# A hybrid encoder layer on one core: the triangular inverses split into halves, and decays from one scan of logarithms

## The chip, the core and the metric

The kernel runs on one core of a Trainium2 chip. A core has a matrix engine (PE, with its weight loads as PEld), three engines for elementwise work (DVE, ACT and POOL), a queue SP that here issues nearly all DMAs, and 16 DMA engines that they share. Each engine takes its instructions strictly in order. The metric is the time of one launch in device microseconds, the median of several runs. Before the change it is 2069.65 us (three runs, 2069.01 to 2072.34).

## The reference, cut to what matters

One layer of a sequence model: 1024 tokens of width 1024, 8 heads of 64 for the part that is changed.

```python
proj = rms_norm(x) @ w_in                       # 6272 columns: rwkv, pooling, attention, gates
y_a = rwkv7_bidir(shifted(p_rwkv), ...)         # below, in both directions e = 0, 1
y_b = multiscale_pool(p_pool, ...)              # four windowed means, each times a 128x128 matrix
y_c = gqa_axial(p_att, ...)
merged = sum of sigmoid(p_gate_b) * (y_b' @ w_branch_b)   # 24 gate blocks of 128 columns
x = x + merged @ w_out
x = x + expert_choice_ffn(rms_norm(x), ...)     # 16 experts
return rms_norm(x)

def step(state, inp):                           # rwkv7_bidir: a scan over the 1024 tokens
    r_t, w_t, k_t, v_t, kk_t, a_t = inp
    sa = einsum('ij,j->i', state, -kk_t)
    state = state * w_t + outer(sa, kk_t * a_t) + outer(v_t, k_t)
    return state, einsum('ij,j->i', state, r_t)
# decay w_t = exp(-exp(-0.5) * sigmoid(w_raw)), a_t = sigmoid(...), k_t = k * (1 + (a_t - 1) * k_a)
```

## The kernel before, in words

The scan over tokens is done in 32 chunks of 32 tokens in each direction. Within a chunk the state's use of earlier tokens is a triangular 32x32 system, and its inverse is worked out beforehand for every chunk, head and direction. Between chunks stands a recurrence of 32 steps, each with three matrix stages.

`projections` comes first. PE forms `proj` in column blocks of 128: `project` needs for a block 48 products of 128x128 by 128x512 (lines 263 to 265: high and low parts), and for each block a weight tile is fetched (SP, line 240), rounded to a high part (ACT, line 257) and its rest formed (DVE, line 258). High and low parts have two buffers each. A string, `PLAN`, sets the order in which the parts are emitted: K, R, V are blocks with a token shift (`shifted`), P is `prep` (decays and the operands of a chunk), C is `products` (the 32x32 matrices, written to `d_a`), O is `pooling`, G one gate block, I `inverses`. A scheduler then orders the instructions of each engine by its own estimate of times. PE's order in the recurrence and in the attention is written by hand; that of DVE, ACT, POOL and SP there is the scheduler's.

`prep` handles 512 tokens of one direction at a time (16 such units). For a unit it forms exp(+d) and exp(-d) of each token's decay on ACT (line 477), makes running products of both by two scans on DVE (lines 482, 484), and corrects the second by a Newton step (lines 494, 495). POOL does affine steps for `a` and `k` (lines 503, 507); in `shifted`, POOL scales a whole block (line 375).

`inverses` solves the triangular systems by back substitution. 128 partitions hold 8 heads of 16 chunks, so four batches hold everything: for each direction e, batch b has every second chunk. Each batch is loaded by 8 DMAs, goes through 31 rows of one multiply (line 597) and one add (line 599), and is stored by 8 DMAs for each engine that took part (line 604, into `d_inv`). The table `INV` gives columns to engines: (0,0) has columns 0 to 10 on DVE and 10 to 32 on POOL, (0,1) and (1,0) are on DVE, (1,1) has 0 to 6 on DVE and the rest on POOL. Every step of the recurrence needs a batch of either parity, so all four come before it. They are emitted at once, at I in the plan, followed by 11 gate blocks and two poolings. `pooling` is a project block, three to four adds on POOL (lines 629, 636), DVE (line 643) and two products on PE (line 648). All of these take their tiles from one pool of 8 (`tmp`).

`gates_and_chain` is the recurrence. Two steps, one for each direction, run side by side. For both: `pr` (line 809), copied by DVE to `R` (line 811); `pu` (line 815), copied to `sv` by DVE and ACT (lines 821, 819); `pf` (line 825), from which DVE makes the next state (line 827). Behind each pair of stages PE runs 5 or 6 products of the remaining gate blocks (line 714), after 62 of them ahead of the first step. `load_pair` fetches the operands of two chunks (lines 784 to 789: `ot`, `tdc`), POOL spreads the inverses into `td` (line 791) and issues the fetch of `sv` (line 776). `rotated` prepares queries and keys, in 22 pieces over the slots 24 to 172 of 192 (six slots are a step of both directions).

Attention and the experts follow, and the change does not touch them.

## Time and profile before

| | |
|---|---|
| median of 3 runs | 2069.65 us |
| the profiled execution | 2065.42 us, span 2063.4 us |
| PE busy | 1900.5 us, 92% of the span |
| DVE, ACT, POOL busy | 1513.7, 1006.6, 645.5 us |
| projections and prep, 37 to 500 us | PE busy 455.23 of 463 us |
| inverses, gates, poolings, 500 to 630 us | PE busy 103.13 of 130 us |
| recurrence, 630 to 930 us | PE busy 290.39 of 300 us |

Times are counted from the start of the span. Idle time of PE is told by "idle before", with what ended it. The granted clock (PEclk) is PE's clock as a share of 2.4 GHz: 1.00 or 0.50. An instruction's time can overlap the next one's on PE, so products are priced by the distance of their starts.

### The profile page before, as it was taken

To read this page: it belongs to the slowest core of one execution; us is meant where nothing else is said; L and a number is where in the kernel's file an instruction comes from. 1 tells how busy PE (TensorE), PEld (TensorE's weight loads), DVE (VectorE), ACT (ScalarE), POOL (GpSimd) and SP (SyncE) were. 2 spreads that over 40 slices of the span, in tenths; PEclk is the share of its full clock that TensorE was granted. 3 is DMA by queue.
4 is the path that set the end of the run, shared out by engine and by line. 5 is a ranking of instruction groups with operands and counts; after the bars stand their busy time and mean duration, and the time that the engine had idled before them with its cause. 6 is when DMAs were issued, how large, how long until landed. Compare 5 with 4: busy or idle time off the path is not lost.

```text
span 2063.4 us, 30617 instructions
## 1 busy us (share of the span) xinstructions
PE 1900.5 (92%) x11324; PEld 1533.8 (74%) x11324; DVE 1513.7 (73%) x2357; ACT 1006.6 (49%) x1477; POOL 645.5 (31%) x659
## 2 busy tenths in 40 slices
PE   6999999998789999989998989995869999999994
PEld 5878777777568888877776768884658888777883
DVE  6485576779833446668987894678969999888896
ACT  4333334241113331238986221333658888877884
POOL 2662353447433333301211476334311000100111
PEclk9999999999899999999999999997989999999997
DMA  4225263484489989960003644547879999995994
GB/s 156 62 72 143 80 159 93 107 211 90 94 178 186 188 160 196 180 174 22 16 17 118 217 130 143 196 181 286 300 267 380 397 381 400 394 369 187 341 384 175
DMA packets 389961, 403.81 MB, mean 196 GB/s; under 512 B 230886, under 2 KB 309300, under 8 KB 389812
## 3 DMA queue, kind: packets, MB, share of 16 engines
q1 hardware_dynamic: 381028, 373.00, 58.7%
q0 software_dynamic: 8784, 28.86, 5.1%
q8 instruction: 89, 1.46, 0.3%
q14 instruction: 60, 0.49, 0.1%
HBM read 325.73 MB, written 76.06 MB: 195 GB/s over the span
## 4 chain that ended last, share of the span: by engine, by line
PE 44%; DVE 8%; issue 5%; ACT 2%; DMA 2%; POOL 2%; SPq 0%; POOLq 0%; DVEq 0%; ACTq 0%
PE mm L714 4%; PE pT L957 3%; PE pg L265 3%; PE pg L263 3%; PE pg L264 2%; PE pf L825 2%; PE mm L263 2%; PE mm L265 2%; PE mm L264 2%; PE pu L263 2%; PE py L264 2%; PE pu L264 2%; PE pu L265 2%; PE py L265 2%; PE py L263 2%
## 5 line engine op out<-in xcount | busy, mean ns | idle before, releaser
L263 PE MATMUL mm<-hn_hi,w_hi 128*128 128x512 f32 x576 | 232.3, 403 | 5.5 <-ACT tmp L366 4.1
L265 PE MATMUL mm<-hn_hi,w_lo 128*128 128x512 f32 x576 | 230.4, 401 | 7.0 <-DVE w_lo L258 7.0
L264 PE MATMUL mm<-hn_lo,w_hi 128*128 128x512 f32 x576 | 231.6, 402 | 0.0
L263 PEld LDWEIGHTS mm<-hn_hi,w_hi 128*128 128x128 f32 x576 | 111.5, 194 | 31.8 <-ACT tmp L366 4.7
L265 PEld LDWEIGHTS mm<-hn_hi,w_lo 128*128 128x128 f32 x576 | 111.3, 193 | 31.0 <-DVE w_lo L258 7.4
L1468 DVE TENSOR_TENSOR lo<-wh,hi 128x1024 fp32r<-128x1024 f32 x103 | 123.3, 1222 | 10.9 <-ACT hi L1459 9.8
L264 PEld LDWEIGHTS mm<-hn_lo,w_hi 128*128 128x128 f32 x576 | 111.3, 193 | 25.6 <-issue 3.1
L1468 DVE TENSOR_TENSOR lo<-wl,hi 128x1024 fp32r<-128x1024 f32 x102 | 122.3, 1227 | 9.7 <-ACT hi L1459 8.7
L257 ACT ACTIVATE w_hi<-w_raw 128x1024 fp32r<-128x1024 f32 x56 | 59.1, 1057 | 136.3 <-PE mm L264 102.5
L1459 ACT ACTIVATE hi<-wh 128x1024 fp32r<-128x1024 f32 x104 | 109.3, 1061 | 32.8 <-PE py L265 16.7
L258 DVE TENSOR_TENSOR w_lo<-w_raw,w_hi 128x1024 fp32r<-128x1024 f32 x56 | 77.6, 1387 | 63.5 <-ACT w_hi L257 63.4
L1459 ACT ACTIVATE hi<-wl 128x1024 fp32r<-128x1024 f32 x104 | 107.6, 1058 | 22.6 <-PE pg L265 10.2
L263 PE MATMUL pg<-hi,xgh 128*128 128x512 f32 x256 | 104.6, 408 | 7.7 <-ACT xgh L1488 7.7
L1530 POOL DMA_INDIRECT d_x<-yo,idx_t x14 | 22.3, 1596 | 278.2 <-ACT yo L1522 277.9
L265 PE MATMUL pg<-hi,xgl 128*128 128x512 f32 x256 | 103.1, 403 | 3.0 <-DVE xgl L1489 2.8
L264 PE MATMUL pu<-lo,xgh 128*128 128x512 f32 x256 | 102.3, 400 | 1.6 <-POOL lo L1466 1.5
L264 PE MATMUL pg<-lo,xgh 128*128 128x512 f32 x256 | 103.4, 404 | 0.5 <-POOL lo L1466 0.4
L263 PE MATMUL pu<-hi,xgh 128*128 128x512 f32 x256 | 101.2, 395 | 1.0 <-DVE hid L1509 1.0
L264 PE MATMUL py<-lo,hidh 128*128 128x512 f32 x240 | 96.4, 402 | 5.9 <-DVE lo L1468 5.6
L265 PE MATMUL pu<-hi,xgl 128*128 128x512 f32 x256 | 100.1, 391 | 0.0
L825 PEld LDWEIGHTS pf<-sv,ot 128*96 128x96 f32 x1024 | 93.7, 166 | 8.1 <-DVE sv L821 1.9
L819 ACT ACTIVATE sv<-pu 32x128 f32<-32x128 f32 x128 | 33.4, 268 | 130.1 <-DVE sv L821 112.1
(422 smaller groups left out, 5359.3 us busy)
## 6 DMA issues: line engine op xcount, KB each, us to landing
w_raw<-in_w_in_dram SPq DMA_DIRECT2D x49, 512.0 KB
wh<-in_exp_up_dram SPq DMA_DIRECT2D x23, 1024.0 KB
wl<-in_exp_up_dram SPq DMA_DIRECT2D x22, 1024.0 KB
wl<-in_exp_down_dram SPq DMA_DIRECT2D x20, 1024.0 KB
wh<-in_exp_down_dram SPq DMA_DIRECT2D x20, 1024.0 KB
mg<-in_exp_gate_dram SPq DMA_DIRECT2D x19, 1024.0 KB
yr<-in_exp_up_dram SPq DMA_DIRECT2D x14, 1024.0 KB
yr<-in_exp_gate_dram SPq DMA_DIRECT2D x13, 1024.0 KB
```

What stands on the lines that cost most here:

```text
L257: nc.scalar.activation(hi, raw, AF.Copy)
L258: nc.vector.tensor_tensor(lo, raw, hi.bitcast(F32), op=ALU.subtract)
L263: nc.tensor.matmul(out, ah, bh, start=start, stop=False)
L264: nc.tensor.matmul(out, ah, bl, start=False, stop=False)
L265: nc.tensor.matmul(out, al, bh, start=False, stop=stop)
L714: nc.tensor.matmul(p, w[:, k, :], x[:, k, ts], start=(k == 0 and n == 0), stop=(k == 7 and n == 2))
L819: nc.scalar.activation(sv[96:128, q::4, :], pu[r], AF.Copy)
L825: nc.tensor.matmul(pf[0:96, q, :], ot[:, q, 0:96], sv[:, q, :], start=True, stop=True)
L957: nc.tensor.transpose(p[:, t * 128:(t + 1) * 128], a, g.ident)
L1459: nc.scalar.activation(hi, raw[:, j], AF.Copy)
L1468: nc.vector.tensor_tensor(lo, raw[:, j], hi.bitcast(F32), op=ALU.subtract)
L1530: nc.gpsimd.indirect_dma_start(out=dst, out_offset=bass.IndirectOffsetOnAxis(ap=chosen(e)[1], axis=0), in_=rows, in_offset=None, compute_o ...
```

## The change

1. `inverses` becomes a generator over batches of half the chunks each: (e, 0) has chunks 0 to 15 and (e, 1) chunks 16 to 31. Direction 0 begins with chunk 0 and direction 1 with chunk 31, so (0,0) and (1,1) are what the first half of the recurrence needs. These two go row by row between the gate blocks of the plan (I1, I5, ...: so many rows). The other two, (0,1) and (1,0), are emitted from within the recurrence, in 33 parts over the slots 2 to 72.
2. `INV`: (1,1) is wholly on DVE; the other three have columns 0 to 10 on DVE and 10 to 32 on POOL.
3. The plan has 12 gate blocks behind I instead of 11, so the recurrence has one block less. `rotated` runs over the slots 76 to 172.
4. `prep` makes one scan, of the sums of the logarithms, and takes exp(+) and exp(-) of it on ACT; the Newton step is gone. Affine steps of POOL go to ACT or into DVE's operations; in `shifted`, ACT writes the scaled block as well.

```diff
-P3 P3 C3 P3 C3 P3 C3 I G G G G G O3 G G G O2 G G G
+P3 P3 C3 P3 C3 P3 C3 I1 G I5 G I5 G I5 G I5 G I6 G I6 G O3 G G G O2 G G
-INV = {(0, 0): [('vector', 0, 10), ('gpsimd', 10, 32)], (0, 1): [('vector', 0, 32)], (1, 0): [('vector', 0, 32)], (1, 1): [('vector', 0, 6), ('gpsimd', 6, 32)]}
+INV = {(0, 0): [('vector', 0, 10), ('gpsimd', 10, 32)], (1, 1): [('vector', 0, 32)],
+       (0, 1): [('vector', 0, 10), ('gpsimd', 10, 32)], (1, 0): [('vector', 0, 10), ('gpsimd', 10, 32)]}
+INV_BEFORE, INV_BESIDE = ((0, 0), (1, 1)), ((0, 1), (1, 0))
+INV0, INV1, N_INV = 2, 72, 33
-ROT1 = 172
+ROT0, ROT1 = 76, 172
+def inverses(g, batches):
...
+    for e, half in batches:
+        um = g.tile4k().rearrange("p (i j) -> p i j", j=32)
+        for q in range(8):
+            nc.sync.dma_start(um[q * 16:q * 16 + 16],
+                              flat(g.d_a[e, half * 16], q * 4096 + CH * 64 + CH, [[8 * 4096, 16], [64, CH], [1, CH]]))
...
+    yield
+    for s in range(31):
+        for e, half, eng, c0, nc_, um, t, X in todo:
...
+            eng.tensor_mul(tv, um[:, isl, j:j + 1].to_broadcast([128, ni, ncl]),
+                           X[:, None, j, csl].to_broadcast([128, ni, ncl]))
+            eng.tensor_add(X[:, isl, csl], X[:, isl, csl], tv)
+        yield
+    for e, half, eng, c0, nc_, um, t, X in todo:
+        for q in range(8):
+            nc.sync.dma_start(flat(g.d_inv[e, half * 16], q % 4 * CH * 64 + q // 4 * CH + c0,
+                                   [[128 * 64, 16], [64, CH], [1, nc_]]), X[q * 16:q * 16 + 16])
+    yield
 # shifted
-            proj(w, t[:, 1:S + 1])
-            nc.gpsimd.tensor_scalar(o, t[:, 1:S + 1], g.c0[:, j:j + 1], None, op0=ALU.mult)
+            def done(p, half):
+                ts = half * 512
+                nc.scalar.activation(t[:, 1 + ts:513 + ts], p, AF.Copy)
+                nc.scalar.activation(o[:, ts:ts + 512], p, AF.Copy, scale=g.c0[:, j:j + 1])
+            project(nc, mmp, hi, lo, w, done)
 # prep
-                for i in range(2):
-                    nc.scalar.activation(wt[:, :, cs], th.rearrange(vch, t=CH), AF.Exp, scale=sgn * EDEC / 2,
...
-                        nc.vector.tensor_tensor_scan(o, wf, d1, 0.0, op0=ALU.mult, op1=ALU.add)
...
-                nc.vector.tensor_mul(nrE, Ein, rE0)
-                nc.vector.scalar_tensor_tensor(nrE, nrE, 2.0, rE0, op0=ALU.subtract, op1=ALU.mult)
+                nc.scalar.activation(wt[:, :, cs], th.rearrange(vch, t=CH), AF.Identity, bias=g.one)
...
+                    nc.vector.tensor_tensor_scan(lg, seg, wf, 0.0, op0=ALU.mult, op1=ALU.add)
...
+                nc.scalar.activation(E, lg, AF.Exp, scale=EDEC / 2)
+                nc.scalar.activation(lg, lg, AF.Exp, scale=-EDEC / 2)
...
-                nc.gpsimd.tensor_scalar(av, ta, 0.5, 0.5, op0=ALU.mult, op1=ALU.add)
-                nc.vector.tensor_mul(av, kkn[:, ts], av)
-                nc.gpsimd.tensor_scalar(kd, ta, g.kah[:, hp:hp + 1], g.kam[:, hp:hp + 1], op0=ALU.mult, op1=ALU.add)
+                nc.scalar.activation(kd, ta, AF.Identity, scale=g.kah[:, hp:hp + 1], bias=g.kam[:, hp:hp + 1])
+                nc.vector.scalar_tensor_tensor(av, ta, 1.0, kkn[:, ts], op0=ALU.add, op1=ALU.mult)
 # gates_and_chain
+        inv = inverses(g, INV_BESIDE)
+        invs = 0
...
+                while invs * (INV1 - INV0) < N_INV * (min(s + 1, INV1) - INV0):
+                    next(inv, None)
+                    invs += 1
```

How the scheduler then places the instructions is seen at three places. Line numbers of the changed kernel are its own: 309 and 311 are the multiply and the add of a row, 630 and 637 the adds of `pooling`, 286 the loads and 315 the stores of the inverses, 791 to 796 the loads of a pair of chunks, 818, 828 and 834 the copies to `R` and `sv` and the next state.

POOL, at the first of the two poolings behind the inverses, before the change:

```order
L597 TENSOR_TENSOR tmp<-tmp 128x48
L599 TENSOR_TENSOR tmp<-tmp 128x24x2
L629 TENSOR_TENSOR tmp<-tmp 128x1055
L597 TENSOR_TENSOR tmp<-tmp 128x69
L636 TENSOR_TENSOR tmp<-tmp 128x1053
L599 TENSOR_TENSOR tmp<-tmp 128x23x3
L636 TENSOR_TENSOR tmp<-tmp 128x1049
```

And the same pooling after it, with the last rows of (0,0) ahead:

```order
L309 TENSOR_TENSOR tmp<-tmp 128x22
L311 TENSOR_TENSOR tmp<-tmp 128x22
L630 TENSOR_TENSOR tmp<-tmp 128x1055
L637 TENSOR_TENSOR tmp<-tmp 128x1053
L637 TENSOR_TENSOR tmp<-tmp 128x1049
L637 TENSOR_TENSOR tmp<-tmp 128x1041
```

The rows of batch (1,1), which stood between the adds of the pooling, are no longer on POOL; the pooling's adds follow each other.

DVE, at the first step of the recurrence, before the change (the copies of both directions follow each other):

```order
L811 COPY R_5359<-pr 128x128
L811 COPY R_5372<-pr 128x128
L821 COPY sv_5225<-pu 32x2x64
L821 COPY sv_5228<-pu 32x2x64
L821 COPY sv_5225<-pu 32x2x64
L821 COPY sv_5228<-pu 32x2x64
L827 TENSOR_TENSOR sv_5348<-pf,Dt 64x512
```

And after it:

```order
L818 COPY R_5129<-pr 128x128
L309 TENSOR_TENSOR tmp<-tmp 128x207
L818 COPY R_5142<-pr 128x128
L311 TENSOR_TENSOR tmp<-tmp 128x23x9
L309 TENSOR_TENSOR tmp<-tmp 128x220
L311 TENSOR_TENSOR tmp<-tmp 128x220
L309 TENSOR_TENSOR tmp<-tmp 128x210
L828 COPY sv_4995<-pu 32x2x64
L311 TENSOR_TENSOR tmp<-tmp 128x210
L309 TENSOR_TENSOR tmp<-tmp 128x200
L828 COPY sv_4995<-pu 32x2x64
```

From the first copy to `R` of step 0 to that of step 1 there are 20 such multiplies and adds on DVE, 20 more to that of step 2, and 6 behind it; then DVE's share of the inverses is done. POOL has 104 of them beside the recurrence, the last ones between the fetches of `sv` for the steps 10 and 11.

SP, ahead of the first step, before the change:

```order
L674 DMA d_sig<-gate 128x512
L240 DMA w_raw<-in_w_in_dram 128x8x128
L674 DMA d_sig<-gate 128x512 x2
L240 DMA w_raw<-in_w_in_dram 128x8x128
L784 DMA ot_5202<-d_ra 64x16x64
L785 DMA ot_5202<-d_a 64x16x64
```

And after it:

```order
L286 DMA tmp<-d_a 16x32x32 x2
L651 DMA d_yb<-tmp 128x1024
L286 DMA tmp<-d_a 16x32x32
L675 DMA d_sig<-gate 128x512
L286 DMA tmp<-d_a 16x32x32 x11
L675 DMA d_sig<-gate 128x512
L286 DMA tmp<-d_a 16x32x32 x2
L240 DMA w_raw<-in_w_in_dram 128x8x128
L791 DMA ot_4972<-d_ra 64x16x64
L792 DMA ot_4972<-d_a 64x16x64
```

The 16 loads for the second halves now stand right ahead of the first pair of chunks, behind the store of the last pooling. On PE, the last products of the 32x32 matrices have 72 products of projections and gates fewer ahead of them than before the change.

## Rows read from the trace of the kernel before

**Rows 1.** Busy time by stretch: us, engines (x instructions), clock, DMA share, GB/s.

```profile
37.00:500.00 463.00, 455.23 (x2930) 365.82 (x2929) 307.78 (x461) 161.46 (x278) 221.30 (x181) 0.97 0.44 113
500.00:630.00 130.00, 103.13 (x453) 81.97 (x452) 76.72 (x181) 21.97 (x34) 54.72 (x92) 0.87 0.63 129
630.00:930.00 300.00, 290.39 (x2888) 243.24 (x2887) 157.18 (x326) 91.30 (x212) 91.11 (x116) 1.00 0.89 180
```

**Rows 2.** Timeline of PE: start, us, instruction, [idle before it <-what ended it].

```profile
509.19 0.79 PE L265 MATMUL mm<-hn_hi,w_lo 128*128 128x512 f32 x1 [7.02 <-DVE w_lo L258]
532.03 0.79 PE L263 MATMUL mm<-hn_hi,w_hi 128*128 128x512 f32 x1 [4.08 <-ACT tmp L366]
559.43 1.19 PE L648 MATMUL sm<-tmp,pw 128*128 128x512 f32 x1 [9.29 <-DVE tmp L643]
580.22 0.67 PE L648 MATMUL sm<-tmp,pw 128*128 128x512 f32 x1 [1.63 <-DVE tmp L643]
618.55 0.33 PE L809 MATMUL pr<-sv,ot 96*32 96x64 f32 x4 [4.48 <-DMA ot<-d_a]
```

**Rows 3.** Stretches right behind four of these, columns as in Rows 1.

```profile
509.20:514.60 5.40, 5.40 (x13) 4.24 (x14) 5.40 (x19) 0.00 (x0) 0.56 (x3) 0.50 0.47 147
532.00:535.20 3.20, 3.17 (x8) 2.50 (x9) 0.00 (x0) 0.46 (x1) 0.00 (x0) 0.50 0.99 165
559.40:562.50 3.10, 3.07 (x5) 1.51 (x5) 2.82 (x9) 0.92 (x2) 1.58 (x5) 0.50 0.00 0
618.60:627.40 8.80, 8.80 (x45) 7.42 (x45) 1.44 (x5) 1.07 (x4) 2.08 (x2) 0.50 1.09 166
```

**Rows 4.** Timeline of PE, two products of gate blocks 45 products apart.

```profile
399.86 0.39 PE L264 MATMUL mm<-hn_lo,w_hi 128*128 128x512 f32 x1
410.06 0.39 PE L264 MATMUL mm<-hn_lo,w_hi 128*128 128x512 f32 x1
```

**Rows 5.** Multiplies of inverse rows (L597): ns min/median/max, first and last start.

```profile
L597 DVE TENSOR_TENSOR tmp<-tmp x102: 115/384/1945, 466.8 to 571.8; 128x60 f32<-128x60 f32 x6, 128x31 f32<-128x31 f32 x5, 128x87 f32<-128x87 f32 x5, 128x112 f32<-128x112 f32 x5
L597 POOL TENSOR_TENSOR tmp<-tmp x56: 228/479/1621, 466.9 to 591.4; 128x88 f32<-128x88 f32 x3, 128x220 f32<-128x220 f32 x2, 128x231 f32<-128x231 f32 x2, 128x240 f32<-128x240 f32 x2
```

**Rows 6.** Timeline of DVE and POOL, rows of 240 to 255 elements.

```profile
484.61 0.82 DVE L597 TENSOR_TENSOR tmp<-tmp 128x240 f32<-128x240 f32 x1
485.24 0.69 POOL L597 TENSOR_TENSOR tmp<-tmp 128x255 f32<-128x255 f32 x1
520.86 0.41 DVE L597 TENSOR_TENSOR tmp<-tmp 128x240 f32<-128x240 f32 x1
```

**Rows 7.** Busy time in the steady recurrence, columns as in Rows 1.

```profile
640.00:880.00 240.00, 237.48 (x2394) 199.43 (x2384) 123.53 (x264) 68.35 (x167) 84.94 (x107) 1.00 0.95 182
```

**Rows 8.** Groups of POOL, same stretch: busy us, mean ns | idle before, releasers.

```profile
L776 POOL DMA_DIRECT2D sv<-d_v x52 | 26.5, 510 | 105.3 <-PE pf L825 60.9 <-PE mm L165 8.3 <-ACT sv L819 7.4
L791 POOL TENSOR_TENSOR td<-tdc,ind 128x512 f32<-128x512 f32 x26 | 26.5, 1036 | 30.0 <-PE pu L815 27.4 <-DMA ot<-d_kb 2.6
```

**Rows 9.** Groups of DVE, same stretch.

```profile
L827 DVE TENSOR_TENSOR sv<-pf,Dt 64x512 f32<-64x512 f32 x52 | 35.4, 682 | 43.7 <-PE pf L825 43.1
L821 DVE COPY sv<-pu 32x128 f32<-32x128 f32 x104 | 28.9, 286 | 38.3 <-PE pu L815 32.3 <-ACT sv L819 4.0
L811 DVE COPY R<-pr 128x128 f32<-128x128 f32 x52 | 13.6, 289 | 17.2 <-PE pr L809 16.9
```

**Rows 10.** Timeline of SP's queue: DMAs that it issues.

```profile
519.31 9.77 SPq L604 DMA_DIRECT2D d_inv<-tmp  x16
604.90 0.93 SPq L784 DMA_DIRECT2D ot<-d_ra  x1
615.60 0.73 SPq L789 DMA_DIRECT2D tdc<-d_inv  x1
```

**Rows 11.** Groups of all engines, 100 to 470 us.

```profile
L375 POOL TENSOR_SCALAR tmp<-tmp,c 128x1024 f32<-128x1024 f32 x10 | 31.8, 3181 | 46.1 <-ACT tmp L366 33.6 <-DVE w_lo L255 12.5
L482 DVE TENSOR_TENSOR_SCAN half<-wseg,d 128x544 f32<-128x544 f32 x16 | 20.1, 1295 | 6.4 <-ACT wseg L477 6.3
```

More of the change, by code (lines that the diff above doesn't have):

```diff
@@ L38 @@
 START_LAG = 0, 0.5, 0.6, 2.6
-INV = {(0, 0): [("vector", 0, 32)], (0, 1): [("vector", 0, 32)], (1, 0): [("vector", 0, 32)],
-       (1, 1): [("vector", 0, 3), ("gpsimd", 3, 32)]}
 SIDE = [(0, 1, 2, 4, 6), (0, 2, 4)]
@@ L143, in make_consts @@
         nc.vector.memset(g.ind2[h * 64:(h + 1) * 64, h:h + 1], 1.0)
-    g.b_dec = c.tile([128, 2], F32, name="b_dec")
-    nc.vector.memset(g.b_dec[:, 0:1], EDEC / 2)
-    nc.vector.memset(g.b_dec[:, 1:2], -EDEC / 2)
+    g.one = c.tile([128, 1], F32, name="one")
+    nc.vector.memset(g.one, 1.0)
     js = c.tile([128, CH], F32, name="js")
@@ L675, in gate, with invert @@
             project(nc, mmp, hi, lo, W.block(3200 + 128 * j), done)
+        inv = inverses(g, INV_BEFORE)
+        def invert(n):
+            for _ in range(n):
+                next(inv, None)
         P = [prep(hp) for hp in range(4)]
@@ L693, in projections @@
             else:
-                {"L": low_rank_in, "B": values, "A": attin, "O": pooling, "I": lambda _: inverses()}[t[0]](i)
+                {"L": low_rank_in, "B": values, "A": attin, "O": pooling, "I": invert}[t[0]](i)
 def gates_and_chain(g, es, hi, lo, W):
```

97 lines of the change are left out of this document (39 added, 58 removed).

## The prediction

> **What bounds the kernel now.** I read the busy time by stretch first. PE is busy 455.23 of 463 us in the projections and 290.39 of 300 us in the recurrence, but 103.13 of 130 us from 500 to 630 us, and there the mean granted clock is 0.87 [rows 1]. So PE sets the pace nearly everywhere, and that stretch is the hole. PE's timeline then names what ended each of its pauses: 7.02 us for a weight rest on DVE (L258), 4.08 us for a tile that ACT writes for a pooling, 9.29 and 1.63 us for the poolings' DVE step (L643), and 4.48 us for the first pair of chunks [rows 2]. The first four have one origin. The inverses stand on DVE from 466.8 to 571.8 us and on POOL from 466.9 to 591.4 us [rows 5]; the splits and the poolings' adds stand among their rows on the same in-order engines, and their tiles come from the same pool of eight. Behind four of the pauses PE works on at a granted clock of 0.50, the 1.2 GHz level, for 5.40, 3.20, 3.10 and 8.80 us [rows 3], having been idle just before; at the upper level the same work takes half of that.
>
> **The ceiling.** The idle time is 7.02 + 4.08 + 9.29 + 1.63 + 4.48 = 26.5 us [rows 2]. The four stretches at half clock are 20.5 us, of which half, 10.25 us, is lost [rows 3]. Together 36.75 us is the most that this stretch can give back.
>
> **First halves between gate blocks.** Before, four batches had to pass before the recurrence; now two do. DVE has one whole batch (62 multiplies and adds) and a tail of (0,0) instead of two and some; POOL has (0,0) alone. The order shows the poolings' adds on POOL behind the last row of (0,0), with no rows among them, and about 20 rows between two splits on DVE where there were up to 35 entries. It also puts the last products of the 32x32 matrices 72 PE products earlier. Two products 45 apart start 10.20 us apart, 0.2267 us each [rows 4], so that is 16.3 us of PE's time earlier for the inverses to begin. A split is needed once in 48 products, 10.9 us. At 0.82 us for a large row that meets POOL's [rows 6], 20 rows and a split take some 17.5 us; at 0.41 us [rows 6] 9.5 us. With two buffers and small rows at both ends that just holds. I let 2 of the first four pauses' microseconds stay. Their 22.0 us and the half-clock loss behind three of them, (5.40 + 3.20 + 3.10) / 2 = 5.85 us, go otherwise: gain 22.0 + 5.85 - 2 = 25.9 us. Bounds: all stays (0), or all goes (27.9).
>
> **The start of the recurrence.** Before, SP issued the first pair's loads from 604.90 us and PE went on at 618.55 us, 13.65 us later [rows 2, 10]. After, the loads stand behind the last pooling's store and 14 of the 16 loads of the second halves. At 9.77 / 16 = 0.61 us per DMA [rows 10] those take 8.5 us, so the first step can start 22.2 us after that store, while PE has 91 products, 20.6 us, left to do. The wait remains of the old kind. I keep the 4.48 us and half of 8.80 us as they are: gain 0, bounds -6 (the loads' data in front on the DMA engines) to +8.9.
>
> **The gate block that moves** from the recurrence to the stretch before it takes 48 x 0.2267 = 10.9 us in either place [rows 4]: 0. PE works at full clock in the recurrence and is busy 237.48 of 240 us there [rows 7], so the steps do become shorter by it.
>
> **Second halves beside the recurrence, DVE.** 52 fetches of `sv`, two a step, make 26 steps in 240 us, 9.2 us each [rows 7, 8]. Of a step's DVE work in its first half, two next states, four copies to `sv` and two to `R` are 2 x 0.682 + 4 x 0.286 + 2 x 0.289 = 3.1 us [rows 9]. The order adds 20 inverse instructions to step 0, 20 to step 1, 6 to step 2. At DVE's median of 0.384 us [rows 5] step 0 has 3.1 + 7.7 = 10.8 us for 9.2; at 0.82 us it has 19.5. The rows shrink through step 1. So the delay is between 0 (rows that get ahead of PE) and 20 us over both; I take 4, near the median's end, because these rows have 30 to 220 elements. What stands behind them on DVE are the copies that PE's next stage waits for, with 5 or 6 products (1.1 to 1.4 us) as their cover.
>
> **POOL.** 104 inverse instructions over some ten steps are about 11 a step. At the median 0.479 us [rows 5] that is 5.3 us, at the 0.69 us of a large row [rows 6] 7.6 us; the fetches and the spreading add (26.5 + 26.5) / 26 = 2.0 us [rows 8]. With 7.3 of 9.2 us it fits, and POOL now waits 105.3 us ahead of its fetches [rows 8], so there is room. Cost 1, bounds 0 to 28 (below).
>
> **SP and the DMA engines.** 48 DMAs of the inverses now fall in or right before the recurrence, where the DMA share is 0.95 already [rows 7]; at 0.61 us they hold SP 29 us, spread over eight steps. The loads of a pair are issued two steps ahead, so most of that is covered: cost 1, bounds 0 to 10. The Trainium skill's page "DMA: Bandwidth & Descriptors" (Specifications) asks for at least 512 B a transfer and says that shorter ones cost a read-modify-write; the new stores have rows of 10 and 22 numbers, 40 and 88 B. By that rule the cost lies towards the upper bound; the trace has such stores (columns 0 to 10 and 10 to 32 of (0,0)) but not next to a busy recurrence.
>
> **prep and shifted.** DVE loses one of two scans (L482: 20.1 us) and two more operations a unit, POOL its scaling (L375: 31.8 us) and two more [rows 11]; ACT gains. PE is busy 455.23 of 463 us there [rows 1], so faster helpers are worth at most 7.8 us; a tighter order of the products could cost as much. I take 0; the use is the earlier start of the inverses, counted above.
>
> **Sum.** -25.9 + 0 + 0 + 4 + 1 + 1 + 0 = -19.9 us. The profiled execution took 2065.42 us and becomes 2045.5; it lies 4.2 us below the median of 2069.65, and with the same distance the forecast is 2050 us, with a range of its own of 2040 to 2060.
>
> **Rivals.**
> *The whole ceiling.* The start finds its loads landed, since SP and POOL are no longer busy with old batches until 591.4 us [rows 5], and the rows beside the recurrence cost nothing: 2069.65 - 36.75 + 2 = 2035 us. Against it stand the 16 loads in front.
> *The pauses return.* Rows on DVE and POOL slow each other as before, the splits stay late, and half of the 27.9 us is kept: -19.9 + 14 = -6, 2064 us. For it: 0.82 against 0.41 us [rows 6]; against it: fewer rows between splits.
> *The recurrence becomes POOL's.* In-order POOL has the fetches of `sv` and the spreading behind its rows. If a row costs more than (9.2 - 2.0) / 11 = 0.65 us, POOL sets the step; SP then waits with the 16 stores of columns 10 to 32, and the next pairs' loads stand behind them. At 0.9 us a step is 11.9 us: 2.7 us more in ten steps, 27 in place of my 1, and 10 for SP in place of 1: -19.9 + 26 + 9 = +15, 2085 us. It turns the sign from about 0.8 us a row. For it: 0.69 us for a row of 255 [rows 6]; against it: the median of 0.479. The Trainium skill, "GPSIMD Engine Reference" (Specifications), says that POOL's way into SBUF is shared with VectorE and contended by its instructions with two SBUF inputs; every inverse row is one. By that rule the split of columns between DVE and POOL gains little and this rival is the likelier; the doubled time of the same row in the trace agrees, while DVE's copies from PSUM lie outside the rule.
>
> **Chances.** Forecast 0.60, whole ceiling 0.15, pauses return 0.13, POOL's recurrence 0.12. A measurement of this kernel tells about 0.2% from no change, so faster is below 2065.5 us and slower above 2073.8. Faster: 0.60 + 0.15 + two thirds of 0.13 = 0.84. Slower: most of the last, 0.10. Same: 0.06. The range reaches into the ceiling's case below and past the returning pauses above: 2034 to 2066 us, with under 0.1 left out on either side.
>
> **What would show it.** Right: no pause of PE over 3 us between the last products and the recurrence's first `pr`, that `pr` near 618.55 - 25.9 + 10.9 = 604 us with one more gate block done, and steps of about 8.9 us (9.2 less 10.9 / 32) behind it; short waits of PE in steps 0 to 2 on DVE's copies to `sv`. Wrong: pauses on L258 or L643 as before; PE waiting for `sv` fetches or `ot` loads through steps 3 to 11; or a loss between 100 and 450 us, where I count none.

## The result and the profile after

The kernel after takes 2043.26 us (median of 4 runs, 2041.89 to 2044.94) against 2069.33 us for the kernel before (4 runs); the ratio is 0.988, with a 95% interval of 0.9865 to 0.9895. The profiled execution took 2044.28 us, span 2042.0 us: 21.1 us less than that of before, where the forecast had 19.9 us, and the median is 6.7 us below the forecast of 2050 us and inside its range. (The forecast carried over the 4.2 us by which the profiled execution of the kernel before lay below its median; that of the kernel after lies 1.0 us above its own.) The total came out nearly as worked out. Its terms did not: three of them are off by 5 to 10 us, and not all to the same side.

To see that, PE's time is split into stages. Idle time is read from gaps of PE over 0.3 us; the loss by half clock is half of PE's busy time in stretches of granted clock 0.50. What is left between 37 us and the first product of attention (`sc`) is 815.5 us in both kernels and 813.7 to 818.3 us in every kernel below, so the two kinds of loss account for nearly all of the differences. Each cell is idle + half clock, in us.

| kernel | 37 to 430 us | 430 us to first `pr` | first `pr` to `sc` | sum | `sc` at |
|---|---|---|---|---|---|
| before | 5.7 + 13.7 | 24.2 + 7.7 | 8.8 + 4.4 | 64.5 | 917.0 |
| after | 2.6 + 10.2 | 1.2 + 0.0 | 14.8 + 14.2 | 43.0 | 895.5 |
| after, again (e9) | 3.8 + 11.1 | 1.4 + 0.9 | 16.5 + 8.5 | 42.1 | 893.4 |
| part 4 alone (e1) | 4.4 + 8.5 | 20.1 + 3.1 | 7.5 + 1.7 | 45.3 | 898.3 |
| halves and plan alone (e2) | 8.9 + 7.1 | 4.6 + 4.6 | 14.1 + 14.2 | 53.4 | 906.6 |
| all batches before (e3) | 3.2 + 11.0 | 16.7 + 7.7 | 6.6 + 3.4 | 48.5 | 900.5 |
| no rows beside (e4) | 3.7 + 11.9 | 6.3 + 1.8 | 20.2 + 7.5 | 51.5 | 902.2 |
| loads behind (e5) | 4.6 + 9.9 | 0.0 + 2.0 | 23.5 + 9.5 | 49.5 | 903.1 |
| loads by ScalarE (e6) | 4.3 + 10.7 | 1.8 + 1.3 | 18.8 + 15.3 | 52.1 | 903.4 |
| 14 products ahead (e7) | 4.3 + 5.1 | 12.2 + 0.0 | 21.9 + 10.4 | 53.9 | 906.5 |
| loads behind, 30 ahead (e8) | 4.3 + 6.8 | 3.6 + 0.0 | 24.1 + 14.5 | 53.3 | 908.6 |
| nothing beside (e10) | 5.7 + 9.9 | 0.0 + 2.0 | 7.1 + 5.1 | 29.9 | 880.9 |
| pooling earlier (e11) | 3.6 + 11.0 | 5.7 + 0.9 | 14.2 + 6.5 | 41.8 | 893.4 |
| one half beside (e12) | 3.6 + 11.9 | 3.8 + 1.8 | 12.5 + 7.5 | 41.0 | 892.9 |

From `sc` on, nothing moved: 917.0 to 2063.4 us before, 895.5 to 2042.0 us after, 1146 us both times (1145 to 1151 us in the kernels below, whose edits do not touch that part). So the 21.5 us are -6.5 in the projections, -30.7 up to the first `pr`, and +15.7 in the recurrence.

The same stages in the view of busy time by stretch of the kernel after. Columns: stretch and its length, busy us (and instructions) of PE, PE's weight loads, DVE, ACT and POOL, mean granted clock, DMA share, GB/s.

```profile
37.00:430.00 393.00, 390.26 (x2604) 312.12 (x2603) 215.18 (x334) 184.88 (x324) 82.82 (x85) 0.97 0.43 114
430.00:586.80 156.80, 155.60 (x746) 126.74 (x743) 68.08 (x157) 34.56 (x49) 65.69 (x98) 1.00 0.53 130
586.80:622.80 36.00, 26.44 (x209) 21.24 (x209) 29.61 (x62) 5.53 (x14) 24.52 (x44) 0.67 1.09 162
622.80:895.50 272.70, 266.35 (x2694) 224.05 (x2682) 145.73 (x315) 77.41 (x188) 112.44 (x168) 0.98 0.91 177
```

The hole of [rows 1], 500 to 630 us, is closed: from 430 us to the first `pr` PE idles 1.2 of 156.8 us, and the four pauses of [rows 2] have no counterpart. A smaller hole has opened behind it: in the first 36 us of the recurrence PE is busy 26.44 us, and that at a mean clock of 0.67, with the DMA share at 1.09 and DVE busy 29.61 us.

PE's timeline shows what ended the waits in it (start, duration, instruction, in brackets the idle time and its releaser). The second line answers to the last of [rows 2].

```profile
586.82 0.43 PE L816 MATMUL pr<-sv,ot 96*32 96x64 f32 x16 [1.20 <-DVE tmp L309]
593.33 0.66 PE L816 MATMUL pr<-sv,ot 96*32 96x64 f32 x16 [6.08 <-DMA ot<-d_a]
607.26 0.43 PE L816 MATMUL pr<-sv,ot 96*32 96x64 f32 x16 [1.09 <-DVE sv L834]
610.48 1.10 PE L822 MATMUL pu<-R,td 128*128 128x64 f32 x8 [1.43 <-DVE R L818]
614.65 5.02 PE L832 MATMUL pf<-sv,ot 128*96 128x64 f32 x28 [0.32 <-DVE sv L828]
625.32 1.08 PE L822 MATMUL pu<-R,td 128*128 128x64 f32 x8 [0.99 <-DVE tmp L309]
849.04 4.43 PE L832 MATMUL pf<-sv,ot 128*96 128x64 f32 x32 [0.91 <-DVE sv L828]
870.51 4.05 PE L832 MATMUL pf<-sv,ot 128*96 128x64 f32 x28 [1.35 <-DVE sv L828]
```

A wait of 6.08 us for the second direction's first pair, four short ones on DVE's results in steps 0 to 2 (each of them behind inverse rows), then almost nothing for 220 us, and two at the end. An L309 named as releaser of PE is an inverse row that PE has no operand from: DVE's counter passed it, and what PE needed must have come later.

The groups of DVE from 593 to 690 us (operation, tiles, count | busy us, mean ns | idle before):

```profile
L311 DVE TENSOR_TENSOR tmp<-tmp 128x207 f32<-128x207 f32 (+22 forms) x23 | 14.5, 631 | 0.6
L834 DVE TENSOR_TENSOR sv<-pf,Dt 64x512 f32<-64x512 f32 x20 | 13.6, 682 | 19.2 <-PE pf L832 19.1
L828 DVE COPY sv<-pu 32x128 f32<-32x128 f32 x40 | 11.5, 287 | 10.4 <-PE pu L822 9.2
L309 DVE TENSOR_TENSOR tmp<-tmp 128x220 f32<-128x220 f32 (+21 forms) x22 | 9.4, 427 | 0.6
L818 DVE COPY R<-pr 128x128 f32<-128x128 f32 x21 | 5.6, 290 | 11.3 <-PE pr L816 11.3
```

The recurrence's own DVE operations take what they took, 682, 287 and 290 ns against 682, 286 and 289 [rows 9], although POOL runs rows beside them. They are not slower, they are later. What makes them later are a few rows. In the mean a row's multiply takes 427 ns and its addition 631 ns, where the forecast took 384 ns, the median of [rows 5]; but most rows are no slower than that: from 586 us on the medians are 334 and 328 ns. Six of these rows take 1.0 to 3.0 us, each while POOL works on rows or spreads inverses. One of them:

```profile
607.13 2.33 DVE L311 TENSOR_TENSOR tmp<-tmp 128x150 f32<-128x150 f32 x1
```

An addition of 140 elements right behind it takes 0.30 us. The long one stands ahead of the copies to `R` that PE waits 1.43 us for at 610.48. A row of 160 elements with 1.69 us (at 604.24) and one of 50 with 2.99 us (at 621.51) stand in the same way ahead of the waits at 607.26 and 625.32. The Trainium skill, "GPSIMD Engine Reference" (Specifications), says that POOL contends with VectorE's instructions that have two SBUF inputs; an inverse row on DVE is one, and the operations fed from PSUM, which kept their times here, are not. The trace agrees on both.

And of POOL in the same stretch:

```profile
L311 POOL TENSOR_TENSOR tmp<-tmp 128x57 f32<-128x57 f32 (+29 forms) x44 | 22.6, 527 | 0.5
L309 POOL TENSOR_TENSOR tmp<-tmp 128x57 f32<-128x57 f32 (+29 forms) x44 | 20.0, 469 | 0.4
L783 POOL DMA_DIRECT2D sv<-d_v x20 | 10.5, 524 | 23.4 <-issue 16.8 <-PE pf L832 5.6 <-ACT y L838 0.5
```

Its rows take 0.47 and 0.53 us, and it still idles 23.4 us in front of its fetches: POOL's own work does not set the pace. Where it acts on it is through the few long rows of DVE beside it; no run has the rows beside the recurrence on one engine alone.

### The profile page after: what moved, and what is told of

Read it like the earlier page. It is cut to its first block, busy times and chain, and to the rows that moved or that the text cites. A ratio compares the mean times of both kernels' runs of the same rounds, so it can differ in the third digit from the quotient of the medians.

```text
span 2042.0 us, 30594 instructions
## 1 busy us (share of the span) xinstructions
PE 1895.8 (93%) x11324; PEld 1531.2 (75%) x11324; DVE 1439.5 (70%) x2265; ACT 1042.8 (51%) x1539; POOL 566.1 (28%) x668
## 5 line engine op out<-in xcount | busy, mean ns | idle before, releaser
L1482 DVE TENSOR_TENSOR lo<-wh,hi 128x1024 fp32r<-128x1024 f32 x103 | 123.2, 1220 | 10.9 <-ACT hi L1473 9.9
L832 PEld LDWEIGHTS pf<-sv,ot 128*96 128x96 f32 x1024 | 98.2, 172 | 10.5 <-DVE sv L828 4.2
L832 PE MATMUL pf<-sv,ot 128*96 128x64 f32 x1024 | 99.3, 256 | 3.2 <-DVE sv L828 2.9
```

The costliest lines, as they stand in the source:

```text
L832: nc.tensor.matmul(pf[0:96, q, :], ot[:, q, 0:96], sv[:, q, :], start=True, stop=True)
L1482: nc.vector.tensor_tensor(lo, raw[:, j], hi.bitcast(F32), op=ALU.subtract)
```

## Experiments

Each ratio is to the kernel before, run beside it on the same chip (four chips in all). Executions of one kernel spread by up to 15 us there, so a ratio is known to about 0.2%, some 4 us. Stages and waits are read from one profiled execution, which need not lie near the median: those of e6, e10 and e12 lie 6.6, 5.1 and 6.2 us above it, those of e5, e7 and e9 6.2, 6.9 and 5.2 us below.

**e1: part 4 without the halves.** The kernel before with the new `prep` and `shifted`, the old inverses and the old plan.

```diff
 # before.py, plus only
+                nc.scalar.activation(E, lg, AF.Exp, scale=EDEC / 2)
+                nc.scalar.activation(lg, lg, AF.Exp, scale=-EDEC / 2)
 # ... and the other lines of shifted and prep of the change
```

> The kernel before with part 4 alone (one scan of logarithms and the affine steps on ScalarE; the inverses and the plan as before). Theory A: the new prep is worth about 10 us by itself, since in 37 to 500 us PE's idle time falls by 5 us and its half-clock time by 10 us; the four pauses from 500 us on stay at 15 to 22 us. Time about 2059 us, ratio 0.995. Rival (the prediction's step): prep is worth nothing there and helps only through an earlier start of the inverses; time 2066 to 2072 us, ratio 0.998 to 1.001, and idle time before 500 us as in the kernel before.

Measured: 2045.38 us, ratio 0.990 (0.9884 to 0.9916). Neither theory had that. By itself part 4 gives about 20 us, as much as the whole change within the noise. The projections of the kernel before by stretch, then the three stages of e1, then e1's PE waits:

```profile
37.00:430.00 393.00, 387.32 (x2411) 310.90 (x2411) 247.58 (x354) 142.13 (x247) 175.53 (x125) 0.97 0.38 104
```

```profile
37.00:430.00 393.00, 388.63 (x2590) 311.19 (x2592) 215.46 (x337) 184.61 (x323) 83.33 (x85) 0.98 0.42 114
430.00:598.10 168.10, 147.96 (x712) 119.75 (x709) 115.04 (x253) 32.83 (x49) 82.77 (x134) 0.94 0.61 130
598.10:898.30 300.20, 291.95 (x2936) 245.55 (x2935) 150.14 (x323) 84.56 (x204) 93.90 (x120) 0.99 0.91 175
```

```profile
487.61 0.79 PE L264 MATMUL mm<-hn_hi,w_lo 128*128 128x512 f32 x1 [6.37 <-DVE w_lo L257]
535.86 3.37 PE L646 MATMUL sm<-tmp,pw 128*128 128x512 f32 x4 [13.77 <-DVE tmp L641]
600.37 0.43 PE L807 MATMUL pr<-sv,ot 96*32 96x64 f32 x16 [1.85 <-DMA ot<-d_a]
```

POOL's work up to 430 us is halved (83 us; before it was 176 us), DVE's falls from 248 to 215 us. PE idles 1.3 us less there, and the first load for the inverses goes out at 405.9 instead of 430.6 us. The pauses stay (20.1 us), but less time is lost at half clock behind them, and with no second halves in the way the recurrence begins almost without a wait.

The mean granted clock is on record for every execution, not only for the profiled one. The span times (1 - clock), an estimate of the time that half clock took (idle time inside such stretches counts in), is 89.1 us in the mean of twelve executions of the kernel before and 76.7 us in six of e1. So some 12 of the 20 us are half clock, as in the table (25.8 against 13.3 us), and some 8 are idle time and order. Which edit of part 4 brings the clock back, and by what way, no run here shows.

**e2: halves and plan without part 4.**

```diff
 # after.py, shifted and prep as in before.py, and
-    g.one = c.tile([128, 1], F32, name="one")
+    g.b_dec = c.tile([128, 2], F32, name="b_dec")
```

> The kernel after with the old prep and shifted (two scans, affine steps on GpSimd); inverses by halves and the plan as after. Theory A: loses the 10 us before 500 us and keeps the rest: about 2053 us, with no pause over 3 us behind the last products. Rival: the inverses need the earlier start that the new prep gives; without it the weight splits come late again, pauses of 5 us and more between the gate blocks, 2058 to 2066 us.

Measured: 2056.71 us, ratio 0.9958 (0.9942 to 0.9974): -9 us, in time between the two theories. In the pauses theory A holds: none over 1.6 us between the gate blocks although the inverses start late (425.5 us), so the rival's mechanism falls. The time that half clock took stays at 87.5 us in the mean of its seven executions. But the recurrence loses 28.3 us by the table, 15 us more than in the kernel before. By the ratios, part 4 alone gives 21 us, the halves alone 9, and both together 19 (e9) to 25 us, not 30.

**e3: all four batches before the recurrence, row by row.**

```diff
-P3 P3 C3 P3 C3 P3 C3 I1 G I5 G I5 G I5 G I5 G I6 G I6 G O3 G G G O2 G G
+P3 P3 C3 P3 C3 P3 C3 I6 G I6 G I6 G I6 G I6 G I6 G I6 G O3 I6 G I6 G I6 G O2 I6 G G
-        inv = inverses(g, INV_BEFORE)
+        inv = itertools.chain(inverses(g, INV_BEFORE), inverses(g, INV_BESIDE))
...
-        inv = inverses(g, INV_BESIDE)
+        inv = inverses(g, ())
```

> The kernel after with all four batches before the recurrence, row by row between all twelve gate blocks (6 rows behind each of the first seven, then 6 in front of three and behind one), none beside the recurrence. Theory row order: what removed the pauses is that rows stand a few at a time between the splits, not that only half of them is there; PE's pauses from 450 to 590 us stay under 4 us in sum, the waits of steps 0 to 2 (4.2 us) and the half clock behind them go, and the time is 2033 to 2041 us. Rival halving: DVE and POOL have too much to do in this stretch (about 105 us of DVE's rows in 125 us beside its splits), the pauses come back at 8 to 20 us, and the time is 2048 to 2062 us.

Measured: 2053.73 us, ratio 0.9942 (0.9924 to 0.9959). The rival holds: 16.7 us of pauses are back.

```profile
498.76 0.79 PE L265 MATMUL mm<-hn_hi,w_lo 128*128 128x512 f32 x1 [4.49 <-DVE w_lo L258]
530.63 0.79 PE L265 MATMUL mm<-hn_hi,w_lo 128*128 128x512 f32 x1 [6.47 <-DVE w_lo L258]
546.75 2.04 PE L649 MATMUL sm<-tmp,pw 128*128 128x512 f32 x2 [5.02 <-DVE tmp L644]
```

Emission row by row is not enough when all four batches stand here; taking two of them out removes the pauses. (In e12 three stand here, the third wholly on DVE, and there are no pauses either.) The recurrence in turn loses only 10.0 us here, with 0.8 us of waiting for `ot`.

**e4: no rows beside the recurrence.** Loads and stores of the second halves stay.

```diff
-            if ncl <= 0:
+            if ncl <= 0 or not rows:
                 continue
...
-        inv = inverses(g, INV_BESIDE)
+        inv = inverses(g, INV_BESIDE, False)
```

> The kernel after with the multiplies and adds of the second halves left out (their loads, memsets and stores stay), so DVE and POOL have no rows beside the recurrence. Theory rows: the rows on DVE hold up the copies that PE waits for in steps 0 to 2; without them the idle time from the first pr to step 3 falls from 4.2 to under 1.5 us, the half-clock stretch of 10.2 us there goes, and the time is 2033 to 2037 us. Rival cover and DMA: the waits come from the thinner cover of gate products and from the loads and stores in front; they stay at 3 us or more and the time is 2041 to 2045 us.

Measured: 2054.93 us, ratio 0.9942 (0.9926 to 0.9957): slower than with the rows. DVE's waits are gone as the first theory says, but without rows the stores are ready at once: four of them pass ahead of the first loads of `ot` in SP's queue, which go out at 588.59 us, and the other 28 stand among the next pairs' loads. PE's waits from 586 to 700 us (total, times, longest):

```profile
PE pr L816 <- DMA ot<-d_a: 20.9, 5, 6.3
PE pf L832 <- ACT sv L826: 1.1, 1, 1.1
```

Of the 20.9 us, 10.9 are waited at the first `pr` and 10.0 from 640 to 665 us. So the loads and stores of the second halves can alone cost more than the rows were to cost, when they come bunched ahead of the `ot` loads: the rival named the cause, and neither had the time.

**e5: the 16 loads behind the first pair's.**

```diff
+        if behind is not None:
+            nc.gpsimd.tensor_copy(um[:, 0, 0:1], behind)
...
-        inv = inverses(g, INV_BESIDE)
+        inv = inverses(g, INV_BESIDE, TD[1, 0][:, 0, 0:1])
```

> The kernel after with the 16 loads of the second halves made to follow the first pair's spread inverses, so that SP issues the loads of the first four pairs (ot, tdc) first. In the kernel after PE stands 1.20 + 6.08 us at the first pr, works 13.7 us at half clock behind it, and has 4.2 us of waits and 10.2 us at half clock in steps 0 to 2. Theory queue: the 16 loads hold SP some 12 us ahead of the ot loads; behind them the first pr waits under 2 us and the half clock behind it goes; 8 to 14 us less, 2030 to 2036 us. The DVE waits of steps 0 to 2 move to the steps where the rows now stand or go. Rival engines: the DMA engines are full at this place whatever the order; the wait stays at 4 us or more; 2040 to 2046 us.

Measured: 2060.3 us (span of the profile 2052.3 us), ratio 0.9972 (0.9958 to 0.9986), against both theories. The wait at the first `pr` is gone (0.70 us), as the first says, and the first 36 us of the recurrence lose 8.1 us instead of 18.4. But what follows loses 24.9 instead of 10.7 us, since the rows start later and now stand among the steps (3.9 of the 24.9 us are a wait of a product of `rotated`). PE's waits from 586 to 700 us:

```profile
PE pr L818 <- DVE sv L836: 7.5, 3, 5.3
PE pf L834 <- DVE sv L830: 3.1, 3, 1.7
PE pr L818 <- DMA ot<-d_a: 0.7, 1, 0.7
```

In the kernel after, the first rows run from 576 us on, while PE still has gate products and then waits for its loads. That wait is partly paid back: it lets the rows get ahead. In e5 they run beside the steps, and beside POOL's largest rows. The longest wait, 5.35 us for a next state of DVE (L836) at 662.53 us, hangs on a single row of 10 elements, which took 4.27 us while nine of POOL's multiplies and adds of 252 to 256 elements ran; the next one of the same size took 0.17 us:

```profile
657.40 4.27 DVE L311 TENSOR_TENSOR tmp<-tmp 128x10 f32<-128x10 f32 x1
661.71 0.17 DVE L313 TENSOR_TENSOR tmp<-tmp 128x10 f32<-128x10 f32 x1
```

The queue theory is right for a part. SP's queue in the kernel after, then in e5 (start, time):

```profile
567.65 7.96 SPq L286 DMA_DIRECT2D tmp<-d_a  x11
575.71 0.63 SPq L675 DMA_DIRECT2D d_sig<-gate  x1
576.38 1.02 SPq L286 DMA_DIRECT2D tmp<-d_a  x2
578.07 1.52 SPq L791 DMA_DIRECT2D ot<-d_ra  x1
```

```profile
569.63 6.45 SPq L677 DMA_DIRECT2D d_sig<-gate  x2
576.98 0.69 SPq L793 DMA_DIRECT2D ot<-d_ra  x1
599.28 7.12 SPq L288 DMA_DIRECT2D tmp<-d_a  x12
```

In both the `ot` loads stand behind a gate block's store of `d_sig`. They go out at 576.98 instead of 578.07 us, which looks like little; but PE is not equally far in the two executions, and what counts is how far ahead of PE the loads go out. PE comes to the first `pr` at 585.62 us in the kernel after (586.82 less its wait of 1.20) and at 588.37 in e5, so the loads have 7.6 us there and 11.4 us here. In the kernel after, ScalarE has the value of that store ready 12.7 us ahead of PE:

```profile
572.34 0.58 ACT L674 ACTIVATE gate<-mm 128x512 f32<-128x512 f32 x1
```

but SP is still busy with the 11 loads, comes to the store 2.8 us later and then issues two more loads. In e5 SP stands waiting when the value is ready, 12.6 us ahead of PE. So the place in SP's queue costs the `ot` loads some 4 us.

**e6: the loads issued by ScalarE.**

```diff
-            nc.sync.dma_start(um[q * 16:q * 16 + 16],
+            (q_eng or nc.sync).dma_start(um[q * 16:q * 16 + 16],
...
-        inv = inverses(g, INV_BESIDE)
+        inv = inverses(g, INV_BESIDE, nc.scalar)
```

> The kernel after with the 16 loads of the second halves issued by ScalarE in place of SyncE, otherwise the same. It tells the place in SP's queue from the traffic: SP comes to the first ot load some 12 us earlier, but the 1 MB in rows of 128 B passes the DMA engines at the same time as before. If the queue is what counts the wait at the first pr (7.3 us with both parts) falls under 2 us, 2030 to 2036 us; if the engines are, it stays over 4 us and the time within 3 us of the kernel after.

Measured: 2045.94 us, ratio 0.9903 (0.988 to 0.9926), the same as the kernel after. PE waits 1.81 and then:

```profile
596.55 0.65 PE L816 MATMUL pr<-sv,ot 96*32 96x64 f32 x16 [5.96 <-DMA ot<-d_a]
```

The numbers are those of the theory of the engines, but the edit does not tell the two apart. The loads now stand on ScalarE, ahead of the gate block's value that SP's store in front of `ot` needs:

```profile
577.26 0.60 ACT L674 ACTIVATE gate<-mm 128x512 f32<-128x512 f32 x1 [7.74 <-DMA tmp<-d_a]
```

So the first `ot` load goes out at 580.80 us, 7.6 us ahead of PE, as in the kernel after. Over all kernels with 62 products ahead of step 0, the wait grows as this lead shrinks (us; the last column is from the issue of the second pair's first load to its `pr`):

| kernels | first `ot` load ahead of PE | waits at the first `pr`, both directions | second pair |
|---|---|---|---|
| e1, e5, e10, e3: none of the 16 loads in front | 11.4, 11.4, 11.4, 11.0 | 1.9, 0.7, 1.0, 0.8 | 8.6, 7.0, 7.1, 7.4 |
| before | 8.4 | 4.9 | 7.1 |
| after, e9, e6, e2: the 16 loads in front | 7.6, 7.0, 7.6, 6.8 | 7.3, 7.1, 7.8, 8.5 | 9.0, 8.5, 9.3, 8.5 |
| e12, e11: stores of `d_inv` in front, too | 6.2, 5.5 | 9.5, 10.9 | 8.7, 8.8 |
| e4 | 0.6 | 10.9 | 7.2 |

Most of the wait is the place in the queues, some 4 of 7 us; the traffic, which makes the loads land later, has at most 2 us.

**e7: 14 products ahead of step 0 in place of 62.**

```diff
-FILL0 = 62
+FILL0 = 14
```

> The kernel after with 14 in place of 62 gate products ahead of step 0, so that the 32 steps have 17.6 products each as before in place of 16.1. Theory cover: the moved gate block has a price, since the last steps wait for DVE's sv copies (0.91 and 1.35 us and two half-clock stretches of 3.4 and 6.8 us that the kernel before does not have); with the old cover they go (5 to 7 us less behind 800 us), while the wait at the first pr grows by up to 10.9 us: 2043 to 2050 us. Rival: cover has no part in it, the waits at the end stay, and the time is 2052 to 2056 us.

Measured: 2061.7 us, ratio 0.9981 (0.9965 to 0.9997); span 2052.9 us. The first `pr` waits as computed, and a wait of step 2 grows:

```profile
583.73 0.66 PE L816 MATMUL pr<-sv,ot 96*32 96x64 f32 x16 [12.21 <-DMA ot<-d_a]
590.02 0.66 PE L816 MATMUL pr<-sv,ot 96*32 96x64 f32 x16 [5.64 <-DMA ot<-d_a]
626.43 0.71 PE L822 MATMUL pu<-R,td 128*128 128x64 f32 x4 [3.69 <-DVE R L818]
```

17.85 us at the first `pr` against 7.28: the 48 products cover 10.6 us of the loads' time. The waits of the last steps stay (0.87, 0.91, 1.04 and 0.94 us), though without half clock behind them; so the thicker cover does not cure them. The span is the rival's; the median is slower than either. The 48 products belong ahead of step 0.

**e8: e5 and 30 products ahead of step 0.**

```diff
-FILL0 = 62
+FILL0 = 30
 # and the edit of e5
```

> Both at once: the loads of the second halves behind the first pairs' and 30 products ahead of step 0 in place of 62. If queue and cover both hold, no wait over 2 us at the first pr, none at the last steps: 2024 to 2030 us, the fastest so far. If only the queue holds: as with the loads behind alone. If the engines are full anyway: the first pr waits 7 us more than there and the time is 2043 to 2052 us.

Measured: 2061.47 us, ratio 0.9976 (0.9964 to 0.9989), with 38.5 us lost in the recurrence. It follows e5: what is saved in front is lost to rows in the steps, and the first `pr` waits 3.16 and 4.33 us.

**e9: the kernel after, again.**

> The kernel after itself once more, as a yardstick for the small differences between the experiments: 0.986 to 0.990 of the kernel before. If it comes out nearer to 0.995, the experiments before it were measured on a chip that is less kind to it, and the difference between it and the kernel with part 4 alone has to be read anew.

Measured: 2046.4 us, ratio 0.9906 (0.9884 to 0.9929). With the first measurement the kernel after stands between 0.988 and 0.991, and e1 with 0.990 between the two. What the halves add to part 4 can't be told from nothing. The time that half clock took is 78.6 us in the mean of the first four executions and 80.4 us in these six, so what part 4 gave back in e1 is given back here too.

**e10: nothing beside the recurrence.** As the expectation says, the second halves are left out.

```diff
+        z = g.tile4k().rearrange("p (i c) -> p i c", c=32)
+        nc.gpsimd.memset(z, 0.0)
+        for e, half in INV_BESIDE:
+            for q in range(8):
+                nc.sync.dma_start(flat(g.d_inv[e, half * 16], q % 4 * CH * 64 + q // 4 * CH,
+                                       [[128 * 64, 16], [64, CH], [1, 32]]), z[q * 16:q * 16 + 16])
...
-        inv = inverses(g, INV_BESIDE)
+        inv = inverses(g, ())
```

> The kernel after with the second halves left out altogether: no rows, loads or stores of them at the recurrence; zeros are stored for them by 16 DMAs early in the projections. It prices everything that stands beside the recurrence. Theory beside: the first pr waits under 2 us, steps 0 to 2 have no wait on DVE, and little half clock follows; of 22.8 us that PE loses in the 42 us from the first pr (10.8 idle, 12 by half clock) 3 to 6 remain: 2024 to 2030 us, ratio 0.979 to 0.983. Rival cover: with the thinner cover and the loads of the first pairs themselves the losses stay at 12 us or more: ratio 0.985 to 0.989.

Measured: 2028.02 us, ratio 0.9815 (0.9792 to 0.9838). Theory beside holds, and in the first 36 us of the recurrence 2.6 us are lost instead of 18.4:

```profile
430.00:589.80 159.80, 159.80 (x808) 130.56 (x807) 64.55 (x128) 37.59 (x55) 61.33 (x83) 0.99 0.53 135
589.80:880.90 291.10, 283.49 (x2887) 238.86 (x2886) 148.96 (x322) 82.90 (x200) 93.61 (x119) 0.98 0.91 177
```

Against e9 on the same chip, what stands beside the recurrence costs 0.9906 - 0.9815 = 0.0091, 19 us with some 7 us either way; by the profiles `sc` is reached 12.5 to 14.6 us earlier without it. The two waits of the last steps (0.91 and 1.35 us) and the half clock behind them remain, so they are not from the second halves. They stand in every kernel with parts 2 and 3 and not in the kernel before and e1, which have one wait of 1.1 us there; the later start of `rotated`, which no run changes by itself, may be behind them.

**e11: the last pooling one gate block earlier.**

```diff
-... O3 G G G O2 G G
+... O3 G G O2 G G G
```

> The kernel after with the last pooling one gate block earlier (O3 G G O2 G G G), so that its tiles come free 10.9 us earlier, the 16 loads of the second halves go out ahead of the first ot loads in time, and DVE's and POOL's large rows of them run while PE still has gate products. Theory head start: rows ahead of the recurrence cost nothing and rows beside it do; the wait at the first pr falls from 7.3 to under 3 us, the waits of steps 0 to 2 under 2 us: 8 to 14 us less than the kernel after, ratio 0.981 to 0.985. Rival ot: the ot loads start when the last tile of the projections comes free, whatever stands ahead of them; ratio 0.987 to 0.990.

Measured: 2045.06 us, ratio 0.9895 (0.9874 to 0.9916). The loads went out 9 us earlier (553.72 us), yet the first `pr` waits 5.68 and 5.20 us. The first `ot` load goes out at 581.98 us, 5.5 us ahead of PE. The gate block in front of it was ready at 574.83, but SP stored it only at 580.79: the first 8 stores of `d_inv` now fall ahead of it (572.76 to 576.80), and behind them SP held a load of `d_att` back for 3.3 us, until a `d_inv` store had landed. The head start brought nothing, as the rival has it in time; but it does matter what stands ahead in the queue.

**e12: one second half beside, one before.**

```diff
-INV_BEFORE, INV_BESIDE = ((0, 0), (1, 1)), ((0, 1), (1, 0))
+INV_BEFORE, INV_NEXT, INV_BESIDE = ((0, 0), (1, 1)), ((0, 1),), ((1, 0),)
-       (0, 1): [('vector', 0, 10), ('gpsimd', 10, 32)], (1, 0): [('vector', 0, 10), ('gpsimd', 10, 32)]}
+       (0, 1): [('vector', 0, 32)], (1, 0): [('vector', 0, 10), ('gpsimd', 10, 32)]}
-        inv = inverses(g, INV_BEFORE)
+        inv = itertools.chain(inverses(g, INV_BEFORE), inverses(g, INV_NEXT))
-... I6 G I6 G O3 G G G O2 G G
+... I6 G I6 G O3 I1 G I8 G I8 G I2 O2 G I7 G I7
```

> The kernel after with one of its two second halves, (0,1), moved ahead of the recurrence, all on DVE, its 33 rows in the last five gate blocks behind the pooling O3, where DVE is busy 26.0 of 93.3 us; only (1,0) stays beside. With nothing beside, the recurrence began and ran 12.5 to 14.6 us quicker. Theory price by batch: half of that comes back, 5 to 9 us less than the kernel after, and PE's pauses from 500 us to the first pr stay under 3 us; ratio 0.984 to 0.987, the fastest of the complete kernels. Rival place: any third batch ahead of the recurrence delays the last pooling and the splits as the four did (16 us of pauses); ratio 0.988 to 0.993. Rival any load: one batch beside costs as much as two, since its loads still stand ahead of the first ot loads; ratio 0.988 to 0.991 with a wait of 5 us at the first pr.

Measured: 2039.85 us, ratio 0.9876 (0.9852 to 0.9901): the lowest ratio of the complete kernels, but not to be told from that of the kernel after. Its third batch costs no pauses, so the rival of place falls. The recurrence loses 20.0 us, between none beside (12.2) and two (25.0 to 29.0): roughly half, as the theory has it. But the wait at the first `pr` stays at 3.80 + 5.67 us, which is what the rival of loads says. Both have a part, and the gain can't be told from the noise.

## Why the prediction came out right, and where it was wrong

*First halves between gate blocks, -25.9.* Right in mechanism and near in size: the stage up to the first `pr` lost 31.9 us before and 1.2 after, -30.7 (2.3 and -29.6 in e9). The 2 us left over for pauses are gone too. e2 shows that it does not need part 4 (9.2 us remain, 3.0 of them the wait at the first `pr`), e3 that four batches row by row do not do it. But what is removed here is mostly paid back in the recurrence: by the table parts 1 to 3 add 2 to 3 us to part 4 alone (sums of 43.0 and 42.1 against 45.3), and by the ratios nothing that can be told. So the term is right, and yet next to part 4 little of it is left over.

*Second halves beside the recurrence, 4 + 1 + 1.* This is the step that failed, by its size. With the start and the moved gate block at 0, the recurrence should have lost 6 us more; it lost 15.7 (11.7 in e9). e10 gives the price of what stands beside directly: 12.5 to 14.6 us by the profiles, 19 with 7 either way by the ratios. The waits were the ones named, on DVE's results in steps 0 to 2, but the price left out three things. It took a median for each row, where the waits hang on a few rows that take 1.0 to 3.0 us beside POOL's work, 4.3 us in e5. It left out PE's half clock behind such waits: in the first 36 us 9.1 us beside 9.3 us of idle time (5.1 beside 11.7 in e9). And it took the loads and stores at 1 of 0 to 10, where e4 waits 20.9 us for `ot` when they come bunched. Rows and transfers don't add up: loads and stores alone, bunched, bring the recurrence to 27.7 us of loss (e4), with the rows to 25 to 29. How the price divides between them in the kernel after stays open.

*The start, 0.* The wait stayed, as predicted: 7.28 us against 4.86 with both directions, within the bounds. The reason given, SP's time for the 16 loads, is right for some 4 us (e5, e6). That the wait grew no more is luck in part: before, the first `ot` load went out 8.4 us ahead of PE, and without the 16 loads the new plan sends it out 11.4 us ahead (e10). The forecast did not count that gain, and the loads took it away again.

*prep and shifted, 0.* Wrong, and by the most. I looked at what PE could gain in 37 to 500 us, at most 7.8 us, and put the earlier start into the first term. Alone part 4 gives 19 us by the profile, 21 by the ratio: 6.4 in the projections, 8.7 up to the first `pr`, 4.1 behind it. Much of that is the same loss that the halves remove, so the two don't add. Next to it, parts 1 to 3 take another 21 to 22 us from the pauses and pay 16 to 20 back in the recurrence. Of the 6.4 us, 5.1 are half clock, which in one profile may be chance (below). Over the whole kernel it is not: by the clocks of all executions part 4 alone gives some 12 us of half clock back (e1). PE's idle time, at which I looked, was the smaller part of what there was to gain.

*The moved gate block, 0.* Nearly: e10 has it before the recurrence and loses 12.2 us there, e1 has it inside and loses 9.2, so at most 3 us for the thinner cover.

*Rivals.* The pauses didn't return, and the recurrence is not POOL's: 0.47 to 0.53 us a row, under the 0.65 from which it would set the step. But the reason given for that rival, contention with DVE, did show, on DVE's rows. The whole ceiling did come in its first part (no pauses), not in its second (a start with its loads landed). The first `pr` came at 586.82 and 593.33 us instead of 604.

So the forecast was met because 4 to 7 us too little gain in each of the two stages before the recurrence stood against 6 to 10 us too little cost in it. That these cancelled is luck.

## What to carry to other kernels

Price work that is moved beside a busy stage by leaving it out there, arithmetic and transfers both: a stage whose engine is 99% busy and whose DMA share is 0.95 [rows 7] has no free room, and short waits cost a quarter to the whole of their length again at half clock (first `pr` to `sc` in the first table). Two edits that remove the same wait don't add, so run each alone before crediting one. Where two engines disturb each other, look at the longest of the small operations and not at their median. And judge the place of a load in a queue by how far ahead of its user it goes out, not by the time of its issue, since two executions are not equally far at the same time.
